# A seven-stage float32 block on one core: GpSimd's adds and most of its low parts go to VectorE, the opening follows the order of arrival, the softmax difference takes one pass

## The chip, the cores and the metric

The kernel runs on one core of one Trainium2 chip. The metric is the device time of one execution in microseconds (us), the median of several; the profile is one further execution with its own time. The engines are TensorE (PE, its weight loads PEld), VectorE (DVE), ScalarE (ACT), GpSimd (POOL) and SyncE (SP), which issues most of the transfers. Each engine works through its own list of instructions in order.

## The reference

One sequence of 256 positions and 1024 channels passes through seven residual stages. Matrix products are computed to float32 accuracy.

```python
h = h + 0.5 * g1 * swiglu(modulate(rmsnorm(h)))          # ffn1, 1024 -> 2816 -> 1024
h = h + g2 * hybrid_mixer(modulate(rmsnorm(h)))          # mixer: conv branch + gated delta rule
h = h + 0.5 * g3 * swiglu(modulate(rmsnorm(h)))          # ffn2
h = rmsnorm(h)
h = h + diff_attention(rmsnorm(h))                       # attn: softmax(a) - lam * softmax(b), 8 heads
h = h + mlp(rmsnorm(h)); h = h + mlstm(rmsnorm(h)); h = h + mlp(rmsnorm(h))
out = rmsnorm(h)
...
p = softmax(logits)                                      # diff_attention, per head
attn = p[:, 0] - lam * p[:, 1]
o = rmsnorm(attn @ v, subln_w) * 0.8                     # eps = 1e-6
```

## The kernel before, in words

`h` stays on chip with channels on the 128 partitions, as 8 tiles of 128x256. The weights (250 MB) stream in as 238 chunks of 1 MB, all issued on SP's queue (line 281), each into one of a few buffers named `raw`. A chunk is two halves of 128x1024. For each half `prep` makes a high part `whi` (ACT, line 320) and a low part `wlo = raw - whi` (line 323). Activations are split the same way (`xh`, `xl`), and each product is three matmuls: high by high (line 407), high weight by low activation (408), low weight by high activation (409). A "unit" is one half: 24 matmuls of 256 columns.

The order of the work on every engine is written out by the code as it runs: nothing is reordered later. `next` hands out a prepared half and prepares halves 2 ahead (4 ahead from `ffn2` on). The low part is recorded one step after the high part, on POOL or DVE: `self.st.pool` is 2 (both halves on POOL), 1 (the first half of each chunk on POOL) or 0 (all on DVE). A few halves at a stage's end (`now`) are always POOL's. Jobs of several steps (the delta rule, an attention core per pair of heads, the bias) sit in `side`; each unit calls `tick`, which takes one step of each job.

At the end of a stage `end_step` adds the products to `h` pair by pair, makes `xh` (ACT) and `xl` (DVE, line 706) for the next stage and squares `h` (ACT, line 625). POOL adds the squares into `ssum` (lines 626 and 628). The next stage starts its products (`unit_first`, line 448 for the `xl` part) before the norm is known; the sum's matmul stands late in the second group (`SUM`), the scale is spread by matmuls (line 668) in the fourth, and until then results are held.

In the mixer `dn_inverse` solves 32x32 triangles by forward substitution: 31 steps of two DVE instructions each (lines 1404 and 1406), two steps to a tick. In attention `combine` (lines 1053 to 1057) forms the difference of two softmaxes per head, and two ticks later `turn` transposes it on PE (line 1063). `h_settle` (line 2013) rescales `h` in eight DVE instructions at one place. In the opening `x` and the vectors come on ACT's queue while SP already loads weights; the norm of `x` must be known before the first product, since `first_ada` scales by it (line 552), and between them DVE reduces the first modulation column (`ada_tile`, line 531).

Of the kernel before, what the change touches and what calls it, by code (L numbers as in the profile page):

```python
# [18 lines left out]
P = 128  # L19
# [348 lines left out]
class Kern:  # L368
# [245 lines left out]
    def sq_start(self):  # L614
        self.ssum = self.work.tile([P, 2, S], F32, tag="ssum", name="ssum", bufs=1)

    def sq_add(self, j):

        nc = self.nc
        h = self.h[:, 2 * j:2 * j + 2]  # L620
        if j == 0:
            nc.scalar.activation(self.ssum, h, AF.Square)
            return
        sq = self.work.tile([P, 2, S], F32, tag="sq", name="sq", bufs=2)
        nc.scalar.activation(sq, h, AF.Square)  # L625
        nc.gpsimd.tensor_tensor(self.ssum, self.ssum, sq, op=ALU.add)  # L626
        if j == KT // 2 - 1:
            nc.gpsimd.tensor_tensor(self.ssum[:, 0], self.ssum[:, 0], self.ssum[:, 1], op=ALU.add)

    def norm_sum(self, parts=None):  # L630

        nc = self.nc
        if self.sqs is not None:
            return self.norm_sum2()
        ps = self.acc2()[:, 0]
        parts = parts or [self.ssum[:, 0]]
        if self.sq_out is not None:
# [113 lines left out]
    def group(self, fn):  # L751

        self.groups += 1
        self.held.append(fn)
        if self.groups <= self.spread_at and self.groups != SUM + 1:
# [260 lines left out]
    def attn_core(self, hp, q, k, bank):  # L1016
# [3 lines left out]
        mx = self.small.tile([P, 2, 4], F32, tag="mx", name="mx")  # L1020
        rec = self.small.tile([P, 2, 4], F32, tag="rec", name="rec")
        o = ap.tile([P, 2, S], F32, tag="o", name="o", bufs=3)
# [27 lines left out]

        def combine(i):
            t = pr[i]
            nc.vector.reciprocal(rec[:, i], sums[:, i])
            for b, c in parts:
                nc.vector.tensor_scalar(t[:, 1, c], t[:, 1, c], rec[:, i, 2 * b + 1:2 * b + 2], self.nlam,  # L1055
                                        op0=ALU.mult, op1=ALU.mult)
                nc.vector.scalar_tensor_tensor(t[:, 0, c], t[:, 0, c], rec[:, i, 2 * b:2 * b + 1], t[:, 1, c],  # L1057
                                               op0=ALU.mult, op1=ALU.add)
# [44 lines left out]
        c = self.small.tile([P, 4], F32, tag="c4", name="c4")  # L1103
        nc.vector.tensor_scalar(m, ms[:, :4], 1.0 / P, EPS, op0=ALU.mult, op1=ALU.add)
        self.rsqrt(c, m, 4)
# [13 lines left out]
    def attention(self, late):  # L1119
        nc = self.nc  # L1120
        x = (self.xh, self.xl)
        with ExitStack() as es:
# [6 lines left out]
            self.late()  # L1129
            self.st.pool = 2  # L1130
            self.v_done, self.down_on = set(), False
# [138 lines left out]
    def dn_keys(self):  # L1270
# [24 lines left out]
        for n in range(10):  # L1295
# [14 lines left out]
            if 1 <= n < 9:  # L1310
# [6 lines left out]
                kk[h] = self.scores(h, self.kqv[0][h // 2])  # L1317
            if n == 8:
                self.hold = False
                self.side.append(self.silu_rest())  # L1320
# [247 lines left out]
    def mixer(self, wide, wide_es, late):  # L1568
        nc = self.nc
        nm = "w_in"  # L1570
        with ExitStack() as es:
            self.mp = mp = es.enter_context(self.tc.tile_pool(name="mix", bufs=1))
            wba = self.work.tile([P, 2, S], F32, tag="sq", name="wba", bufs=2)[:, 0].rearrange("p (k c) -> p k c", k=KT)
            nc.scalar.dma_start(wba, self.arg["w_ba"])
            wb = self.work.tile([P, 2, S], F32R, tag="sq", name="wb", bufs=2).rearrange("p a (k c) -> p a k c", k=KT)
            wbh, wbl = wb[:, 0], wb[:, 1]
            self.zs = mp.tile([P, KT, S], F32, name="zs")
# [7 lines left out]
            for n in range(NLATE):  # L1585
# [12 lines left out]
                if n == 1:  # L1598
                    self.st.pool = 1
                if n == 3:  # L1600
# [13 lines left out]
            with self.tc.tile_pool(name="mix1", bufs=4) as m1:  # L1614
# [27 lines left out]
                def chain():  # L1642
# [3 lines left out]
                    self.side.append(self.dn_queries())  # L1646

                for r in (1, 0, 2):
                    for hp in range(4):
# [11 lines left out]
                self.tick_first = False  # L1661
                self.st.pool = 1
                for n in range(0, 8, 2):
# [213 lines left out]
    def mlstm(self, late):  # L1877
# [3 lines left out]
        with ExitStack() as es:  # L1881
# [78 lines left out]
            for n in range(8):  # L1960
# [6 lines left out]
                self.group(lambda ps=ps, c=4 * i + h, out=qk[h][i]: conv(ps, c, out))  # L1967
                if n == 1:
                    self.st.pool = 1
                if n == 3:  # L1970
# [5 lines left out]
            for h in range(4):  # L1976
                self.st.pool = 1
# [29 lines left out]
    def h_settle(self):  # L2007
# [3 lines left out]
        self.unsettled = False  # L2011
        for k in range(KT):
            self.nc.vector.scalar_tensor_tensor(self.h[:, k], self.h[:, k], self.vec("norm_final", k, 1), self.r1,
                                                op0=ALU.mult, op1=ALU.mult)

# [5 lines left out]
    def run(self):  # L2021
# [17 lines left out]
        c = self.small.tile([P, KT], F32, tag="c", name="c")  # L2039
        nc.sync.dma_start(c, arg["c"])  # L2040
        nc.scalar.dma_start(self.consts[:, :P], arg["consts"][:, :P])
        nc.scalar.dma_start(self.h, arg["x"])
        nc.scalar.dma_start(self.vecs, arg["vecs"])
# [6 lines left out]
        if "ffn1" in st:  # L2050
            self.zeros = self.first.tile([P, S], F32, name="zeros")
            nc.gpsimd.memset(self.zeros, 0.0)
            self.cold = self.acc2()[:, 0]
            self.warm(5)
        pc = [self.up(2 * S) for _ in range(2)]
# [3 lines left out]
        if "ffn1" in st:  # L2059
            sq = self.first.tile([P, 4, 2, S], F32, name="sq1")  # L2060
            h = self.h.rearrange("p (j a) s -> p j a s", a=2)
            for j in range(2):
                nc.scalar.activation(sq[:, j], h[:, j], AF.Square)
                nc.vector.tensor_tensor(sq[:, j + 2], h[:, j + 2], h[:, j + 2], op=ALU.mult)
            for j in (2, 0):
                nc.vector.tensor_tensor(sq[:, j], sq[:, j], sq[:, j + 1], op=ALU.add)
            for j in range(2):
# [5 lines left out]
            self.scale0 = self.first_scale()  # L2073
            self.norm_sum([sq[:, j, i] for j in (2, 0) for i in range(2)])
            self.warm(3)
# [157 lines left out]
```

## Time and profile before

| | |
|---|---|
| median of 3 runs | 1389.32 us (1383.68 to 1390.25) |
| the profiled execution's own time | 1393.07 us |
| its span (first to last instruction) | 1391.3 us |
| PE / DVE / ACT / POOL busy | 1339.4 / 979.2 / 665.9 / 202.0 us |
| mean granted TensorE clock | 0.980 of full speed |

Busy time is the union of an engine's instructions. A PE that is busy at half clock counts as busy, so the gap between PE's busy time and the span is not all that PE loses.

### The profile page before, as it was taken

The page shows a single profiled execution, that of the slowest core. Times are in us where ns is not written, and L with a number is a line of the kernel's source. Part 1 is how long each engine was busy: PE and PEld are TensorE (multiplying, and loading weights), DVE is VectorE, ACT ScalarE, POOL GpSimd, SP SyncE. Part 2 cuts the span into 40 slices and gives each one's busy share as a digit, 9 for nine tenths or more (in the row PEclk, how much of TensorE's full clock was granted, in tenths as well). Part 3 has the DMA queues.
Part 4 walks back from the last instruction along what each step waited for, and adds up shares of the span by engine and source line. Part 5 has one row for each costly group of instructions (what it writes and reads, how often), then busy time and mean ns, then how long its engine had stood idle before and what let it go on. Part 6 is the DMA issues. An engine that isn't in the chain of part 4 may idle for free.

```text
span 1391.3 us, 26555 instructions
## 1 busy us (share of the span) xinstructions
PE 1339.4 (96%) x11102; PEld 1312.1 (94%) x11102; DVE 979.2 (70%) x1757; ACT 665.9 (48%) x1052; POOL 202.0 (15%) x107
## 2 busy tenths in 40 slices
PE   8999999999989899999999989999999999999997
PEld 7999998999889899999999979999999899999997
DVE  6987778688797476965445886876665958866664
ACT  3544445657534435544445445544444664544442
POOL 0000004246224001000001653100000330100000
PEclk8999999999989999999999989999999999999998
DMA  8988763454547425486554432455555344455550
GB/s 326 360 298 305 305 275 113 137 179 152 152 156 216 175 89 185 156 318 213 186 185 139 147 121 100 153 181 182 182 183 182 122 152 167 145 204 182 182 182 31
DMA packets 44968, 257.97 MB, mean 185 GB/s; under 512 B 12520, under 2 KB 12784, under 8 KB 14256
## 3 DMA queue, kind: packets, MB, share of 16 engines
q1 hardware_dynamic: 34704, 250.10, 50.6%
q10 hardware_dynamic: 9760, 4.84, 1.6%
q8 instruction: 87, 1.43, 0.4%
q0 software_dynamic: 384, 1.32, 0.3%
q14 instruction: 33, 0.27, 0.1%
HBM read 254.14 MB, written 2.11 MB: 184 GB/s over the span
## 4 chain that ended last, share of the span: by engine, by line
PE 59%; DVE 8%; issue 0%; ACT 0%; DVEq 0%
PE up L407 10%; PE up L409 10%; PE up L408 10%; PE acc L407 7%; PE acc L409 7%; PE acc L408 7%; DVE xl L706 1%; DVE lt L1055 1%; PE acc L1523 1%; DVE wlo L323 1%; DVE lt L1057 1%; PE acc L668 1%; DVE xwl L706 0%; DVE h L833 0%; DVE rs_i L501 0%
## 5 line engine op out<-in xcount | busy, mean ns | idle before, releaser
L320 ACT CAST whi<-raw 128x1024 fp32r<-128x1024 f32 x404 | 420.7, 1047 | 437.4 <-PE up L408 184.3
L407 PE MATMUL up<-xh,whi 128*128 128x256 f32 x1744 | 504.7, 289 | 1.1 <-ACT xh L723 0.6
L409 PE MATMUL up<-xh,wlo 128*128 128x256 f32 x1744 | 497.3, 285 | 8.3 <-DVE wlo L323 8.3
L408 PE MATMUL up<-xl,whi 128*128 128x256 f32 x1744 | 497.0, 285 | 1.2 <-DVE xl L1720 1.1
L323 DVE TENSOR_TENSOR wlo<-raw,whi 128x1024 fp32r<-128x1024 f32 x337 | 420.4, 1258 | 68.4 <-ACT whi L320 66.5
L409 PEld LDWEIGHTS up<-xh,wlo 128*128 128x128 f32 x1744 | 337.6, 194 | 9.6 <-DVE wlo L323 9.5
L407 PEld LDWEIGHTS up<-xh,whi 128*128 128x128 f32 x1744 | 337.6, 194 | 3.9 <-issue 1.2
L408 PEld LDWEIGHTS up<-xl,whi 128*128 128x128 f32 x1744 | 337.6, 194 | 3.1 <-DVE xl L1720 1.3
L323 POOL TENSOR_TENSOR wlo<-raw,whi 128x1024 fp32r<-128x1024 f32 x67 | 164.9, 2463 | 667.3 <-ACT whi L320 657.2
L407 PE MATMUL acc<-gh,whi 128*128 128x256 f32 x864 | 244.7, 283 | 0.0
L409 PE MATMUL acc<-gh,wlo 128*128 128x256 f32 x864 | 244.6, 283 | 0.0
L408 PE MATMUL acc<-gl,whi 128*128 128x256 f32 x864 | 244.6, 283 | 0.0
L407 PEld LDWEIGHTS acc<-gh,whi 128*128 128x128 f32 x864 | 165.9, 192 | 0.6 <-issue 0.6
L408 PEld LDWEIGHTS acc<-gl,whi 128*128 128x128 f32 x864 | 165.9, 192 | 0.0
L409 PEld LDWEIGHTS acc<-gh,wlo 128*128 128x128 f32 x864 | 165.9, 192 | 0.0
L955 DVE TENSOR_TENSOR t<-up,rs 128x256 f32<-128x256 f32 x60 | 25.4, 423 | 103.5 <-PE up L409 103.5
L531 DVE SCALAR_TENSOR_TENSOR raw<-raw,crow 128x1024 f32<-128x1024 f32 x72 | 87.9, 1250 | 2.1 <-DMA raw<-in_stream 2.0
L882 DVE TENSOR_TENSOR gf<-up,sa 128x256 f32<-128x256 f32 x35 | 14.6, 423 | 79.2 <-PE up L409 79.2
L626 POOL TENSOR_TENSOR ssum<-ssum,sq 128x512 f32<-128x512 f32 x15 | 20.5, 1369 | 266.2 <-ACT sq L625 265.5
L878 ACT ACTIVATE sa<-up 128x256 f32<-128x256 f32 x35 | 13.3, 384 | 53.9 <-PE up L409 50.5
L407 PE MATMUL up<-whi,xh 128*128 128x256 f32 x128 | 38.8, 303 | 0.0
L408 PE MATMUL up<-wlo,xh 128*128 128x256 f32 x128 | 37.4, 292 | 0.0
(482 smaller groups left out, 1955.7 us busy)
## 6 DMA issues: line engine op xcount, KB each, us to landing
raw<-in_stream SPq DMA_DIRECT2D x238, 1024.0 KB, 5.0
h<-in_x ACTq DMA_DIRECT2D x1, 1024.0 KB, 8.4
bflip<-bdram POOLq DMA_DIRECT2D x1, 1024.0 KB, 6.7
d<-c ACTq DMA_DIRECT2D x1, 512.0 KB, 2.8
m<-d ACTq DMA_DIRECT2D x4, 128.0 KB, 7.0
d<-x ACTq DMA_DIRECT2D x1, 512.0 KB, 3.4
xd<-d ACTq DMA_DIRECT2D x4, 128.0 KB, 4.7
out_h<-h SPq DMA_DIRECT2D x2, 256.0 KB, 2.7
```

Of the source, the lines that this page charges most:

```text
L320: nc.scalar.copy(hi[:, :n], raw)
L323: self.lows.append(lambda: eng.tensor_tensor(lo[:, :n], raw, hi[:, :n].bitcast(F32), op=ALU.subtract))
L407: t.matmul(ps, lhsT=wh, rhs=xh, start=start, stop=False, skip_group_check=True)
L408: t.matmul(ps, lhsT=wh, rhs=xl, start=False, stop=False, skip_group_check=True)
L409: t.matmul(ps, lhsT=wl, rhs=xh, start=False, stop=stop, skip_group_check=True)
L531: self.nc.vector.scalar_tensor_tensor(w, w, 1.0, self.crow, op0=ALU.mult, op1=ALU.mult, accum_out=self.mods[:, c:c + 1])
L626: nc.gpsimd.tensor_tensor(self.ssum, self.ssum, sq, op=ALU.add)
L668: self.nc.tensor.matmul(ps[:, c0 + b * P:c0 + (b + 1) * P], lhsT=tok[:, b:b + 1].to_broadcast([P, P]), rhs=self.const("ident"), start=True ...
L706: nc.vector.scalar_tensor_tensor(x[1][:, k, :S], self.h[:, k], a[:, k:k + 1], x[0][:, k, :S].bitcast(F32), op0=ALU.mult, op1=ALU.subtract)
L882: product(n, lambda gf: None, lambda gf: nc.vector.tensor_tensor(gf, ps, sa, op=ALU.mult))
L955: nc.vector.tensor_tensor(t, src, self.rs, op=ALU.mult)
L1055: nc.vector.tensor_scalar(t[:, 1, c], t[:, 1, c], rec[:, i, 2 * b + 1:2 * b + 2], self.nlam, op0=ALU.mult, op1=ALU.mult)
```

## The change

The lambda of the softmax difference is multiplied by the ratio of the two sums, so that one pass forms the difference times the first sum; the factor is taken out by the norm that follows, whose eps is multiplied by that sum squared (`ep`). The squares of `h` are kept in four tiles (the fourth in PSUM) and added on DVE after the next stage's first group. `pool` is set only for the three q, k, v runs of the mixer (1), within `dn_keys` (2) and back to 0 at its ninth step. `h_settle` becomes a side job. In the opening `x` comes as two halves on SP's queue ahead of the weights, the squares and their sums follow the halves, and the first run of idle matmuls has 3 instead of 5. The small transfer `w_ba` is issued two groups later, since its buffer is one of the square tiles.

```diff
     def sq_add(self, j):
...
-        nc.gpsimd.tensor_tensor(self.ssum, self.ssum, sq, op=ALU.add)
-        if j == KT // 2 - 1:
-            nc.gpsimd.tensor_tensor(self.ssum[:, 0], self.ssum[:, 0], self.ssum[:, 1], op=ALU.add)
+        sq = self.ssum
+        if j == 3:
+            sq = self.acc2()
+        elif j:
+            sq = self.work.tile([P, 2, S], F32, tag="sq", name="sq", bufs=2)
+        self.nc.scalar.activation(sq, self.h[:, 2 * j:2 * j + 2], AF.Square)
+        self.sq_parts.append(sq)
+
+    def sq_sum(self):
...
+        add = lambda a, b: self.nc.vector.tensor_tensor(a, a, b, op=ALU.add)
+        a, b, c, d = self.sq_parts
...
+        add(a, b)
+        add(c, d)
+        add(a, c)
+        add(a[:, 0], a[:, 1])
...
         self.held.append(fn)
+        if self.groups == 1:
+            self.sq_sum()
...
         def combine(i):
...
-            nc.vector.reciprocal(rec[:, i], sums[:, i])
+            one = sums[:, i, 0:4:2]
+            nc.vector.reciprocal(rec[:, i], sums[:, i, 1:4:2])
+            nc.vector.scalar_tensor_tensor(rec[:, i], rec[:, i], self.nlam, one, op0=ALU.mult, op1=ALU.mult)
+            nc.vector.scalar_tensor_tensor(ep[:, i], one, EPS, one, op0=ALU.mult, op1=ALU.mult)
             for b, c in parts:
-                nc.vector.tensor_scalar(t[:, 1, c], t[:, 1, c], rec[:, i, 2 * b + 1:2 * b + 2], self.nlam,
-                                        op0=ALU.mult, op1=ALU.mult)
-                nc.vector.scalar_tensor_tensor(t[:, 0, c], t[:, 0, c], rec[:, i, 2 * b:2 * b + 1], t[:, 1, c],
+                nc.vector.scalar_tensor_tensor(t[:, 0, c], t[:, 1, c], rec[:, i, b:b + 1], t[:, 0, c],
                                                op0=ALU.mult, op1=ALU.add)
...
-        nc.vector.tensor_scalar(m, ms[:, :4], 1.0 / P, EPS, op0=ALU.mult, op1=ALU.add)
+        nc.vector.scalar_tensor_tensor(m, ms[:, :4], 1.0 / P, ep.rearrange("p a b -> p (a b)"),
+                                       op0=ALU.mult, op1=ALU.add)
...
-            self.st.pool = 2
             self.v_done, self.down_on = set(), False
...
             if n == 8:
+                self.st.pool = 0
                 self.hold = False
...
+                self.st.pool = 1
                 for r in (1, 0, 2):
...
-                self.st.pool = 1
                 for n in range(0, 8, 2):
...
-        for k in range(KT):
-            self.nc.vector.scalar_tensor_tensor(self.h[:, k], self.h[:, k], self.vec("norm_final", k, 1), self.r1,
-                                                op0=ALU.mult, op1=ALU.mult)
+
+        def settle():
+            for k in range(KT):
+                self.nc.vector.scalar_tensor_tensor(self.h[:, k], self.h[:, k], self.vec("norm_final", k, 1), self.r1,
+                                                    op0=ALU.mult, op1=ALU.mult)
+                yield
+        self.side.append(settle())
...
+        for j in range(2):
+            nc.sync.dma_start(self.h[:, 4 * j:4 * j + 4], arg["x"][:, 4 * j:4 * j + 4])
         nc.scalar.dma_start(self.consts[:, :P], arg["consts"][:, :P])
-        nc.scalar.dma_start(self.h, arg["x"])
...
-            self.warm(5)
+            self.warm(3)
```

How the lists of the engines change is seen at three places. Of the 67 low parts that POOL made, 17 stay there; DVE has 387 in place of 337.

The first place is DVE's list at the seam between attention and the first mlp, before: `h` and `xl` pair by pair, then low parts and the norm.

```order
L833 TENSOR_TENSOR h<-acc,h 128x512
L706 SCALAR_TENSOR_TENSOR xl<-h,vecs,xh 128x256 x4
L323 TENSOR_TENSOR wlo<-raw,whi 128x1024 x3
L644 TENSOR_SCALAR nm<-acc 128x2
L501 TENSOR_SCALAR rs_i<-nm 128x2
```

And of the change:

```order
L846 TENSOR_TENSOR h<-acc,h 128x512
L717 SCALAR_TENSOR_TENSOR xl<-h,vecs,xh 128x256 x4
L323 TENSOR_TENSOR wlo<-raw,whi 128x1024 x2
L632 TENSOR_TENSOR ssum<-ssum,sq 128x512
L632 TENSOR_TENSOR sq<-sq,acc 128x512
L632 TENSOR_TENSOR ssum<-ssum,sq 128x512
L632 TENSOR_TENSOR ssum<-ssum 128x256
L323 TENSOR_TENSOR wlo<-raw,whi 128x1024
L655 TENSOR_SCALAR nm<-acc 128x2
```

The four adds moved behind all of `xl` and two low parts, ahead of the norm; before, POOL made them while DVE made `xl`.

The second place is DVE's list in the middle of the forward substitution, before (`tmp` and `x` are its two instructions of a step, `ct` belongs to the convolution branch):

```order
L1406 TENSOR_TENSOR x<-x,tmp 128x16x16
L323 TENSOR_TENSOR wlo<-raw,whi 128x1024
L1404 TENSOR_TENSOR tmp<-m,x 128x255
L1406 TENSOR_TENSOR x<-x,tmp 128x15x17
L1404 TENSOR_TENSOR tmp<-m,x 128x252
L1406 TENSOR_TENSOR x<-x,tmp 128x14x18
L1691 TENSOR_TENSOR ct<-up,cc 128x256
L1404 TENSOR_TENSOR tmp<-m,x 128x247
```

And of the change:

```order
L1423 TENSOR_TENSOR x<-x,tmp 128x16x16
L323 TENSOR_TENSOR wlo<-raw,whi 128x1024
L1421 TENSOR_TENSOR tmp<-m,x 128x255
L1423 TENSOR_TENSOR x<-x,tmp 128x15x17
L1421 TENSOR_TENSOR tmp<-m,x 128x252
L1423 TENSOR_TENSOR x<-x,tmp 128x14x18
L1707 TENSOR_TENSOR ct<-up,cc 128x256
L323 TENSOR_TENSOR wlo<-raw,whi 128x1024
L1421 TENSOR_TENSOR tmp<-m,x 128x247
```

Between the first and the last of the 31 steps DVE now has 13 low parts, where it had 6.

The third place is DVE's list in attention where a pair of heads is combined, before (`rec` are reciprocals of the sums, `lt` the exponentials):

```order
L1156 TENSOR_TENSOR k<-up,rs 128x256
L1053 RECIPROCAL rec<-sums 128x4
L1055 TENSOR_SCALAR lt<-lt,rec,nlam 128x128
L1057 SCALAR_TENSOR_TENSOR lt<-lt,rec 128x128
L1055 TENSOR_SCALAR lt<-lt,rec,nlam 128x256
L1057 SCALAR_TENSOR_TENSOR lt<-lt,rec 128x256
```

And of the change:

```order
L1172 TENSOR_TENSOR k<-up,rs 128x256
L323 TENSOR_TENSOR wlo<-raw,whi 128x1024
L1069 RECIPROCAL rec<-sums 128x2
L1070 SCALAR_TENSOR_TENSOR rec<-rec,nlam,sums 128x2
L1071 SCALAR_TENSOR_TENSOR ep<-sums 128x2
L1073 SCALAR_TENSOR_TENSOR lt<-lt,rec 128x128
L1073 SCALAR_TENSOR_TENSOR lt<-lt,rec 128x256
```

Two passes over 128x128 and 128x256 are gone, two instructions on 128x2 are new, and a low part stands in nearly every unit.

## Rows read from the trace of the kernel before

**Rows 1.** The page, part 1: busy us, share of the span, instructions.

```profile
PE 1339.4 (96%) x11102; PEld 1312.1 (94%) x11102; DVE 979.2 (70%) x1757; ACT 665.9 (48%) x1052; POOL 202.0 (15%) x107
```

**Rows 2.** Waits of PE, whole span: us in total, times, longest.

```profile
PE up L409 <- DVE wlo L323: 9.3, 8, 4.2
PE acc L1063 <- DVE lt L1057: 5.8, 3, 3.8
...
PE acc L448 <- DVE xl L706: 3.1, 3, 1.0
PE acc L448 <- DVE xwl L706: 2.8, 4, 1.1
```

**Rows 3.** Waits of PE in 380 to 400, 400 to 420 and 1080 to 1120 us.

```profile
PE up L409 <- DVE wlo L323: 4.2, 1, 4.2
...
PE up L409 <- DVE wlo L323: 2.1, 1, 2.1
...
PE acc L668 <- DVE rtok L515: 1.6, 1, 1.6
```

**Rows 4.** Timeline: start, us, engine, line, operation; POOL's rows and DVE's.

```profile
801.03 2.41 POOL L323 TENSOR_TENSOR wlo<-raw,whi 128x1024 fp32r<-128x1024 f32 x1 [0.30 <-ACT whi L320]
...
801.12 2.47 DVE L1055 TENSOR_SCALAR lt<-lt,rec,nlam 128x256 f32<-128x256 f32 x1
...
847.22 0.41 DVE L1055 TENSOR_SCALAR lt<-lt,rec,nlam 128x256 f32<-128x256 f32 x1
...
888.68 0.87 DVE L706 SCALAR_TENSOR_TENSOR xl<-h,vecs,xh 128x256 fp32r<-128x256 f32 x2
889.47 0.68 DVE L833 TENSOR_TENSOR h<-acc,h 128x512 f32<-128x512 f32 x1
890.07 4.79 DVE L706 SCALAR_TENSOR_TENSOR xl<-h,vecs,xh 128x256 fp32r<-128x256 f32 x4
...
890.32 4.26 POOL L626 TENSOR_TENSOR ssum<-ssum,sq 128x512 f32<-128x512 f32 x3 [31.54 <-ACT sq L625]
```

**Rows 5.** Line 323 by source, DVE's group: ns min/median/max, first and last start.

```profile
L323 DVE TENSOR_TENSOR wlo<-raw,whi x337: 1202/1219/3422, 20.4 to 1365.1; 128x1024 fp32r<-128x1024 f32 x169
```

**Rows 6.** Timeline of DVE: first and last of seven in 363 to 416 us, of eighteen in attention.

```profile
363.95 2.38 DVE L1404 TENSOR_TENSOR tmp<-m,x 128x31 f32<-128x31 f32 x1
...
412.04 2.30 DVE L1406 TENSOR_TENSOR x<-x,tmp 128x60 f32<-128x60 f32 x1
...
764.00 1.46 DVE L660 TENSOR_SCALAR nm<-nm 128x2 f32<-128x2 f32 x1
...
856.51 2.41 DVE L1057 SCALAR_TENSOR_TENSOR lt<-lt,rec 128x128 f32<-128x128 f32 x1
```

**Rows 7.** Windows: us, busy of PE, PEld, DVE, ACT, POOL, granted clock, DMA.

```profile
363.00:416.00 53.00, 46.70 (x349) 45.96 (x348) 49.39 (x93) 21.13 (x34) 17.48 (x7) 0.90 0.45 159
756.00:864.00 108.00, 99.96 (x751) 95.20 (x750) 83.74 (x167) 52.26 (x125) 55.36 (x23) 0.92 0.38 127
...
559.90:563.40 3.50, 3.50 (x16) 3.50 (x17) 3.34 (x3) 0.73 (x1) 0.00 (x0) 0.51 0.41 96
805.70:812.50 6.80, 6.20 (x28) 5.48 (x29) 6.66 (x18) 0.48 (x1) 0.27 (x1) 0.50 0.46 154
833.00:836.40 3.40, 3.09 (x14) 2.80 (x15) 2.12 (x6) 0.48 (x1) 0.00 (x0) 0.50 0.21 89
10.40:20.60 10.20, 8.92 (x31) 7.91 (x32) 7.49 (x30) 2.96 (x6) 0.00 (x0) 0.50 0.91 350
```

**Rows 8.** The opening: transfers with us to landing, then timeline rows.

```profile
h<-in_x ACTq DMA_DIRECT2D x1, 1024.0 KB, 8.4
...
13.01 1.22 DVE L531 SCALAR_TENSOR_TENSOR raw<-raw,crow 128x1024 f32<-128x1024 f32 x1
15.29 0.16 DVE L644 TENSOR_SCALAR nm<-acc 128x2 f32<-128x2 f32 x1 [1.05 <-PE acc L641]
20.83 0.39 PE L407 MATMUL acc<-xh,whi 128*128 128x256 f32 x1
```

More of the change, by code (lines that the diff above doesn't have):

```diff
@@ L615, in sq_start @@
         self.ssum = self.work.tile([P, 2, S], F32, tag="ssum", name="ssum", bufs=1)
+        self.sq_parts = []
     def sq_add(self, j):
[L619 to L622, printed above, removed]
-            return
-        sq = self.work.tile([P, 2, S], F32, tag="sq", name="sq", bufs=2)
-        nc.scalar.activation(sq, h, AF.Square)
-        nc.gpsimd.tensor_tensor(self.ssum, self.ssum, sq, op=ALU.add)
-        if j == KT // 2 - 1:
-            nc.gpsimd.tensor_tensor(self.ssum[:, 0], self.ssum[:, 0], self.ssum[:, 1], op=ALU.add)
+        sq = self.ssum
[6 more added lines that the diff above has]
+    def sq_sum(self):
+        if len(self.sq_parts) < 4:
+            return
+        add = lambda a, b: self.nc.vector.tensor_tensor(a, a, b, op=ALU.add)
+        a, b, c, d = self.sq_parts
+        self.sq_parts = []
+        add(a, b)
+        add(c, d)
+        add(a, c)
+        add(a[:, 0], a[:, 1])
     def norm_sum(self, parts=None):
@@ L754, in group @@
         self.held.append(fn)
+        if self.groups == 1:
+            self.sq_sum()
         if self.groups <= self.spread_at and self.groups != SUM + 1:
@@ L1020, in attn_core @@
         mx = self.small.tile([P, 2, 4], F32, tag="mx", name="mx")
-        rec = self.small.tile([P, 2, 4], F32, tag="rec", name="rec")
+        rec = self.small.tile([P, 2, 2], F32, tag="rec", name="rec")
+        ep = self.small.tile([P, 2, 2], F32, tag="ep", name="ep")
         o = ap.tile([P, 2, S], F32, tag="o", name="o", bufs=3)
@@ L1572, in mixer @@
             self.mp = mp = es.enter_context(self.tc.tile_pool(name="mix", bufs=1))
[L1573 to L1576, printed above, removed]
             self.zs = mp.tile([P, KT, S], F32, name="zs")
@@ L1598, in mixer @@
                 if n == 1:
-                    self.st.pool = 1
+                    wba = self.work.tile([P, 2, S], F32, tag="sq", name="wba", bufs=2)[:, 0].rearrange("p (k c) -> p k c", k=KT)
+                    nc.scalar.dma_start(wba, self.arg["w_ba"])
+                    wb = self.work.tile([P, 2, S], F32R, tag="sq", name="wb", bufs=2).rearrange("p a (k c) -> p a k c", k=KT)
+                    wbh, wbl = wb[:, 0], wb[:, 1]
                 if n == 3:
@@ L1661, in mixer @@
                 self.tick_first = False
-                self.st.pool = 1
                 for n in range(0, 8, 2):
@@ L1967, in mlstm @@
                 self.group(lambda ps=ps, c=4 * i + h, out=qk[h][i]: conv(ps, c, out))
-                if n == 1:
-                    self.st.pool = 1
                 if n == 3:
@@ L1976, in mlstm @@
             for h in range(4):
-                self.st.pool = 1
                 pv = self.unit_wide(nm, x)
@@ L2061, in run @@
             h = self.h.rearrange("p (j a) s -> p j a s", a=2)
[L2062 to L2066, printed above, removed]
+            nc.scalar.activation(sq[:, 0], h[:, 0], AF.Square)
+            nc.vector.tensor_tensor(sq[:, 1], h[:, 1], h[:, 1], op=ALU.mult)
+            nc.vector.tensor_tensor(sq[:, 0], sq[:, 0], sq[:, 1], op=ALU.add)
+            nc.scalar.activation(sq[:, 2], h[:, 2], AF.Square)
+            nc.vector.tensor_tensor(sq[:, 3], h[:, 3], h[:, 3], op=ALU.mult)
+            nc.vector.tensor_tensor(sq[:, 2], sq[:, 2], sq[:, 3], op=ALU.add)
             for j in range(2):
@@ L2073, in run @@
             self.scale0 = self.first_scale()
-            self.norm_sum([sq[:, j, i] for j in (2, 0) for i in range(2)])
+            self.norm_sum([sq[:, j, i] for j in (0, 2) for i in range(2)])
             self.warm(3)
```

## The prediction

> **What bounds the kernel now.** I read the page first: PE is busy for 96% of the span and DVE for 70% [rows 1]. So the matmuls are the bound, and a change that leaves them alone can only give back what PE loses between them. That loss has two parts. The first is PE's waits. The view of waits names DVE behind most of them: for low parts 9.3 us, for the softmax difference 5.8, for the low parts of the new activations at the stage seams 3.1 and 2.8 [rows 2]. The second is the granted clock: after such waits there are stretches in which PE runs at 1.2 GHz instead of 2.4 [rows 7], and each us of them does half a us of work.
>
> DVE has 30% of its time free, so why is it late? The timeline answers. POOL starts a low part at 801.03 and needs 2.41 us; DVE starts a pass over 128x256 at 801.12, and it ends when POOL's ends, after 2.47 us [rows 4]. The same form takes 0.41 us at 847.22, beside no POOL work [rows 4]. At the seam behind attention two `xl` instructions take 0.87 us together, and the last four, beside POOL's three adds, 4.79 [rows 4]. A DVE instruction that reads its operands from SBUF and meets a POOL instruction there is held until POOL has finished. DVE is in order, so all behind it is late too. I take that as the mechanism: in 363 to 416 us seven DVE instructions are stretched so, by 12.5 us over their plain forms, and in attention eighteen, by 30.4 us [rows 6]. A low part costs DVE 1.22 us when it makes it itself [rows 5], half of what it can lose to POOL's.
>
> **The change part by part**, against the profiled execution's own 1393.07 us (span 1391.3).
>
> *Opening.* The last product before the steady run waits for the norm of `x`. `x` lands 8.4 us after its issue, the sums' result is used at 15.29, and the first product starts at 20.83 [rows 8]. Transfers ran at 350 GB/s [rows 7]. `x` shared this with the weights on SP's queue, so about 2.1 MB had to move before its last byte, 6.0 us, which leaves 2.4 us of start. Placed first on SP's queue it shares with constants and vectors alone, 1.05 + 0.38 MB, 4.1 us: an estimate of 6.5 in place of 8.4, 1.9 us earlier. The first half's square and add now lie beside the second half's transfer, so two of four DVE passes of about 0.68 us [rows 4] are out of the chain: 1.4 more. The first weight chunk comes later than before, 3.0 us behind `x`, at about 9.5 from the issue; DVE's pass over it, now at 13.01 [rows 8], still starts earlier. I take 3.3. The low end is 1: the clock is at 1.2 GHz from 10.4 to 20.6 us [rows 7] after PE had idled, and products that start sooner may start at that clock. The high end is 5, if `x` gets most of the rate. By the Trainium skill (TensorE: Matmul & The Clock Gate, What's actually happening) the gate throttles by default and activity releases it, which speaks against dropping two of the five idle matmuls; no row here shows a start with three, and by this rule the term would be at its low end.
>
> *Seams.* Five seams lose POOL's adds. Each had one wait of about 1.0 us for the last `xl`: three are the 3.1, two are in the 2.8, whose two other waits are short [rows 2]. The last four `xl` took 4.79 us where twice 0.87 is 1.74 [rows 4], so the last lands 3 us sooner and PE does not wait: 5.0 (3 to 5.9, which is all of both rows). The adds return as three passes of 0.68 and one of half that on DVE, 2.4 us, behind `xl` and ahead of the norm. That is less than the 3.0 freed just before, so the norm is not later; without that cover it would cost up to 2.4 at each seam. They wait for ACT's last square, which ACT makes straight behind the last `xh`; queued behind them are a low part two units ahead of its use and the norm. At the mLSTM's seam POOL also holds a DVE low part, and PE waits 1.6 us for the norm [rows 3]; I take 1.6 (0 to 1.6). Of the 9.3 us for low parts, 3.0 are small waits at other places, most behind a held DVE; I take 2 (0 to 3).
>
> *Substitution, 363 to 416 us.* DVE is busy for 49.39 of 53 us [rows 7], and PE waits 4.2 and 2.1 for low parts [rows 3]. Seven low parts come to DVE here, 7 x 1.15 = 8.0 us, and 12.5 us of holding go. DVE gains 4.5 us and PE follows DVE here, so I take 4.5. The bounds: -2, if half of the holding stays, and 6.3, both waits.
>
> *Attention, 756 to 864 us.* DVE is busy for 83.74 of 108 us [rows 7]. 23 low parts come, 23 x 1.15 = 26.4; the eight combines lose a pass over 128x256 (0.41, [rows 4]) and one over half of it, and gain two tiny instructions, about 3 us saved in all; 30.4 of holding go. That leaves about 77 us of DVE work for some 96 us of PE work, and the transposes have two ticks of slack behind the combine. Of the 5.8 us I take 5 (1 to 5.8). The eight `h_settle` instructions, one by one, cost the same DVE time; before, they stood as one block ahead of a combine.
>
> *Clock.* The stretches of 3.5, 6.8 and 3.4 us at 1.2 GHz [rows 7] follow the waits at the mixer's end and in attention that I take away: 13.7 us at half speed, 6.9 us of work. Not each goes with its wait; I take 5 (0 to 6.9). That of the substitution I leave out, as DVE is the bound there.
>
> *Nothing* for the earlier or later place of `w_ba` (one small transfer, two groups ahead of its use) and for squares written to PSUM: ACT is busy for 48% [rows 1].
>
> Sum: 3.3 + 5.0 + 1.6 + 2 + 4.5 + 5 + 5 = 26.4, to 1366.7 by the profiled execution. The median lies 3.75 below that execution, so I predict 1389.3 - 26.4 = 1363 us. The low ends add up to 3 us, the high ends to 34.5.
>
> **The rivals.**
>
> *DVE turns slow by its own load.* Where DVE is nearly full, the low parts only change their reason to be late: substitution and attention gain nothing, nor does the clock, and the opening, the seams and the mLSTM's norm give 9.9: 1379 us. For it speaks that DVE gets 50 low parts, 57 us, into stretches that are 93% and 78% full, and that low parts now stand ahead of the combine in DVE's list. Against it: the holding is larger than the load in both.
>
> *DVE becomes the bound, slower.* If the stretched instructions were late for a reason that stays, attention would hold 83.74 + 26.4 - 3 = 107 us of DVE work; with half of its old idle time, 12, that is 119 for 108, and the substitution 49.4 + 8 + 3.6 of idle = 61 for 53. Nineteen us lost against 9.9 gained: 1398. It decides once less than 64% of the holding goes in the substitution (8.0 of 12.5) and about three quarters in attention (23 of 30.4). For this speaks a rule of the Trainium skill (Perfetto Trace Analysis, Optimizing Scalar/DVE Operations): with DVE saturated, moving work to ScalarE or even GpSimd may make sense. The same section adds that the two share a read port and that it might not help, and that is what rows 4 show. So I give it little.
>
> *All goes.* The high ends give 34.5. If the substitution then runs at full clock too, 53 us at a granted 0.90 [rows 7] give another 5.3: about 1350. For it speaks that most waits have one cause; against it, that DVE stays 80% full in attention and in order.
>
> *The softmax difference does nothing by itself*: 3 us of DVE work in attention are hidden unless DVE is the bound there; it is no term of its own.
>
> **How the numbers follow.** Forecast, 1353 to 1372: 0.55. DVE slow by its own load, 1372 to 1383: 0.22. All goes, below 1353: 0.13. Slower: 0.05. No change for reasons that I don't see: 0.05. The range 1346 to 1379 leaves out the slower case, no change, half of the "all goes" and a part of the first rival, about 0.2. A measurement of this kernel can tell 0.5%, 7 us, from no change. Faster than that: 0.87 (the forecast, "all goes", most of the first rival); within it: 0.08; slower: 0.05.
>
> **What would show it.** Right: no DVE instruction at a seam or in attention above its plain length; POOL with 17 low parts; the first product near 17.5 us; no wait of PE for `xl` at the five seams; waits for `lt` under 1 us; fewer stretches at half clock. Wrong: DVE over 90% busy in attention, with PE waiting for `wlo` there; the substitution as long as before; the first product at 20 us, with `x` landed early but the first chunk of weights late. The prediction fails if DVE is not late because of POOL, or if the half clock stays where it is.

## Result and the profile after

| | before | after |
|---|---|---|
| median | 1388.34 us (1383.68 to 1390.25) | 1355.38 us (1355.24 to 1355.85) |
| profiled execution's own time / its span | 1393.07 / 1391.3 us | 1355.85 / 1354.1 us |
| mean granted TensorE clock | 0.980 | 0.989 |

The ratio is 0.9768 [0.9743, 0.9793]: 33 us less by the medians, 37.2 us less by the two spans. The forecast was 1363.

The page, part 1, of the kernel after (as [rows 1]):

```profile
PE 1320.2 (97%) x11098; PEld 1297.7 (96%) x11098; DVE 968.4 (72%) x1827; ACT 666.3 (49%) x1052; POOL 57.1 (4%) x37
```

DVE has 70 instructions more and is busy 11 us less, although it took over 50 low parts and the adds. Most of the stretching that was counted as its busy time is gone. Counted over the whole span are DVE's instructions that overlap one of POOL and last over 0.2 us longer than the median of the same form away from POOL: 63 before, 84.5 us above that median, and 13 after, 9.4 us. Of these 13, eight lie beside POOL's copies `L` at 412 to 422 us, in the mixer (2.8 us); no run here moves those copies.

To see where the time came from I split the executions at PE's landmarks: the first product of each stage, the first matmul of the mixer's gates (`pre_i`), the last matmul of its solve, the last transpose of a `turn`. Lengths in us, worked out from start times in the timeline; the four columns on the right are experiments told below.

| stretch | before | after | low parts alone | attention's back | mixer's back | adds back |
|---|---|---|---|---|---|---|
| start to first product | 20.8 | 16.9 | 20.7 | 16.7 | 16.5 | 15.9 |
| mixer to its gates | 53.7 | 48.0 | 50.2 | 48.0 | 52.1 | 51.6 |
| gates to the last solve (substitution, mixer's end) | 198.8 | 189.1 | 189.6 | 191.7 | 197.8 | 188.6 |
| ffn2 to attention | 200.9 | 198.2 | 200.9 | 198.2 | 198.2 | 199.6 |
| attention to the last turn | 110.0 | 96.7 | 97.1 | 103.0 | 96.7 | 93.7 |
| mlp0 to mLSTM | 186.9 | 187.1 | 186.9 | 187.1 | 187.1 | 186.9 |
| mLSTM to mlp1 | 116.6 | 114.5 | 114.3 | 114.5 | 114.5 | 114.3 |
| mlp1 to the last matmul | 192.7 | 192.9 | 192.7 | 192.9 | 193.2 | 192.6 |

Two of these stretches in the view of windows (columns as in [rows 7]), first of before, the mixer's middle and attention:

```profile
267.92:466.74 198.82, 185.07 (x1795) 178.07 (x1794) 150.41 (x301) 108.72 (x189) 79.02 (x39) 0.97 0.53 175
750.75:860.80 110.05, 102.01 (x769) 97.27 (x768) 85.36 (x167) 56.69 (x132) 55.36 (x23) 0.92 0.35 117
```

The same two of after:

```profile
258.24:447.33 189.09, 181.46 (x1795) 174.74 (x1795) 153.83 (x318) 108.91 (x189) 39.87 (x22) 0.98 0.55 181
728.61:825.33 96.72, 96.30 (x769) 93.15 (x768) 77.44 (x190) 56.74 (x132) 0.00 (x0) 0.96 0.42 139
```

In attention the same 769 matmuls now run with 0.4 us of idle PE in place of 8.0, and the clock is granted at 0.96 in place of 0.92. DVE has 23 instructions more there and is busy 7.9 us less.

The opening after, as in [rows 8] (transfers, then timeline rows):

```profile
h<-in_x SPq DMA_DIRECT2D x2, 512.0 KB, 5.4
...
10.23 1.23 DVE L531 SCALAR_TENSOR_TENSOR raw<-raw,crow 128x1024 f32<-128x1024 f32 x1 [0.98 <-DMA raw<-in_stream]
11.39 0.15 DVE L655 TENSOR_SCALAR nm<-acc 128x2 f32<-128x2 f32 x1
16.89 0.38 PE L407 MATMUL acc<-xh,whi 128*128 128x256 f32 x1
```

The sums are used at 11.39 instead of 15.29, and the first product starts at 16.89 instead of 20.83.

Not everything went. The longest waits of PE, whole span (as [rows 2]):

```profile
PE acc L652 <- DVE ssum L632: 3.4, 3, 1.1
PE acc L444 <- DVE h L850: 3.3, 2, 1.7
PE up L407 <- ACT whi L320: 3.1, 1, 3.1
```

The waits for `xl` at the seams (5.9 us in two lines of [rows 2]) are gone, and the first two lines here, 6.7 us, stand at the same five seams: for the sum at the three without a gate, for `h` at the two with one (behind ffn1 and the mixer, where the products are multiplied by a gate as they are added to `h`). DVE's timeline at the seam into mlp0 shows the first kind (compare [rows 4], where the last four `xl` took 4.79):

```profile
854.61 1.66 DVE L717 SCALAR_TENSOR_TENSOR xl<-h,vecs,xh 128x256 fp32r<-128x256 f32 x4
857.64 2.36 DVE L323 TENSOR_TENSOR wlo<-raw,whi 128x1024 fp32r<-128x1024 f32 x2 [1.37 <-ACT whi L320]
859.92 0.69 DVE L632 TENSOR_TENSOR ssum<-ssum,sq 128x512 f32<-128x512 f32 x1
...
861.96 0.42 DVE L632 TENSOR_TENSOR ssum<-ssum 128x256 f32<-128x256 f32 x1
```

`xl` is done 3.1 us sooner, but the next in DVE's list is a low part whose high part ACT has not made: DVE stands idle for 1.37 us, then makes two low parts, and only then adds the squares, the last of which ACT had finished at 856.64.

### The profile page after: what moved, and what is told of

It is laid out like the page before. It is cut to its first block, busy times and chain, and to the rows that moved or that the text cites. A ratio compares the mean times of both kernels' runs of the same rounds, so it can differ in the third digit from the quotient of the medians.

```text
span 1354.1 us, 26498 instructions
## 1 busy us (share of the span) xinstructions
PE 1320.2 (97%) x11098; PEld 1297.7 (96%) x11098; DVE 968.4 (72%) x1827; ACT 666.3 (49%) x1052; POOL 57.1 (4%) x37
## 4 chain that ended last, share of the span: by engine, by line
PE 84%; DVE 9%; ACT 3%; issue 1%; DMA 1%; ACTq 1%; SPq 0%; DVEq 0%
PE up L407 16%; PE up L409 16%; PE up L408 16%; PE acc L407 9%; PE acc L408 9%; PE acc L409 9%; DVE wlo L323 3%; DVE raw L531 1%; PE acc L1278 1%; PE acc L1540 1%; PE acc L679 1%; ACT xh L713 1%; ACT whi L320 1%; DVE ssum L632 0%; ACTq L1430 0%
## 5 line engine op out<-in xcount | busy, mean ns | idle before, releaser
L323 DVE TENSOR_TENSOR wlo<-raw,whi 128x1024 fp32r<-128x1024 f32 x387 | 470.1, 1224 | 68.2 <-ACT whi L320 66.1
L323 POOL TENSOR_TENSOR wlo<-raw,whi 128x1024 fp32r<-128x1024 f32 x17 | 41.0, 2416 | 389.9 <-ACT whi L320 383.8
L891 ACT ACTIVATE sa<-up 128x256 f32<-128x256 f32 x35 | 13.3, 384 | 50.9 <-PE up L409 47.5
L407 PE MATMUL acc<-yh,whi 128*128 128x256 f32 x128 | 36.4, 284 | 0.0
```

Source lines behind the costliest of these rows:

```text
L323: self.lows.append(lambda: eng.tensor_tensor(lo[:, :n], raw, hi[:, :n].bitcast(F32), op=ALU.subtract))
L407: t.matmul(ps, lhsT=wh, rhs=xh, start=start, stop=False, skip_group_check=True)
```

## The experiments

**Theory.** A GpSimd instruction that reads SBUF holds VectorE's until it ends, and that is most of the loss (A). **Rivals:** attention's gain comes from the softmax difference and the spread `h_settle` (B); the low parts only change their reason to be late and the rest of the change does the work (C). Ratios are to the kernel before; the changed kernel's 0.9768 is the yardstick.

### The low parts alone

On the kernel before, only the numbers of `pool` changed (the comments are added here; the second removed number stood at four places):

```diff
-            self.st.pool = 2          # attention
...
             if n == 8:
+                self.st.pool = 0
...
-                    self.st.pool = 1  # mixer's first product, gb, mLSTM
+                self.st.pool = 1      # mixer's q, k, v
```

> The kernel before with only the low parts moved from GpSimd to VectorE as in the changed kernel; opening, seam adds, softmax difference and h_settle stay as before. Theory A (a GpSimd instruction holds VectorE's, and that is most of the loss): the mixer between its opening gates and its end gives back about 13 us and attention about 12, so 1361 to 1366 us. Theory B (attention's gain comes from the softmax difference in one pass and from h_settle being spread out): only the mixer's part, 1373 to 1378 us. Theory C (the low parts only change their reason to be late, the rest of the change does the work): 1383 to 1389 us.

1364.50 us, ratio 0.9816 [0.9799, 0.9832]. As A has it (1361 to 1366): 50 low parts that change their engine give 25.8 us, where the whole change gives 33. Attention falls to 97.1 us with the old softmax difference and the old block of `h_settle`. Windows, attention:

```profile
737.81:834.89 97.08, 96.66 (x770) 93.49 (x769) 80.93 (x190) 56.85 (x132) 0.00 (x0) 0.96 0.40 136
```

C falls with this run, and so does B as it stands: attention's gain is there without the softmax difference and the spread `h_settle`.

### Attention's low parts back on GpSimd

```diff
+            self.st.pool = 2
             self.v_done, self.down_on = set(), False
```

> The changed kernel with attention's low parts back on GpSimd (pool = 2 there, one line). Theory A: attention's stretched VectorE instructions come back, and with them about 10 to 13 us: 1365 to 1369 us, with the turns' waits for lt and half-clock stretches in attention. Theory B: the softmax difference already relieves VectorE, so 0 to 3 us are lost: 1355 to 1359 us.

1363.47 us, 0.9806 [0.9792, 0.9821], between what A and B said. Windows, attention:

```profile
730.75:833.79 103.04, 98.72 (x770) 94.83 (x769) 79.97 (x167) 56.63 (x132) 55.62 (x23) 0.95 0.37 125
```

103.0 us: 6.3 more than the changed kernel, but 7.0 less than before, and A said 10 to 13. With the low parts on POOL the shorter `combine` and the spread `h_settle` do count; this run does not tell the two apart. The view of waits has 1.9 us for `lt` in place of 5.8.

### The softmax difference in two passes

```diff
...
-                nc.vector.scalar_tensor_tensor(t[:, 0, c], t[:, 1, c], rec[:, i, b:b + 1], t[:, 0, c],
+                nc.vector.tensor_scalar(t[:, 1, c], t[:, 1, c], rec[:, i, 2 * b + 1:2 * b + 2], self.nlam,
+                                        op0=ALU.mult, op1=ALU.mult)
+                nc.vector.scalar_tensor_tensor(t[:, 0, c], t[:, 0, c], rec[:, i, 2 * b:2 * b + 1], t[:, 1, c],
...
```

> The changed kernel with the softmax difference in two passes as before (reciprocals of all four sums, plain eps in the norm). Theory A: VectorE has room in attention once nothing holds it, so the 3 us of passes are hidden: 1355 to 1357 us, the same within the measurement. Theory B: the turns wait for lt again: 1363 to 1368 us.

1353.31 us, 0.9733 [0.9719, 0.9748], no slower than the changed kernel, and 1.7 us below the range that A gave. Windows, attention:

```profile
727.80:822.96 95.16, 94.74 (x770) 91.59 (x769) 80.96 (x190) 56.73 (x132) 0.00 (x0) 0.98 0.40 139
```

DVE is busy 3.5 us more and PE still idles 0.4. The 1.6 us in which attention is shorter go with the granted clock, 0.98 to 0.96.

### The mixer's low parts back on GpSimd

```diff
             if n == 8:
-                self.st.pool = 0
...
                 if n == 1:
+                    self.st.pool = 1
...
-                self.st.pool = 1
...
                 self.tick_first = False
+                self.st.pool = 1
```

> The changed kernel with the mixer's low parts back on GpSimd as before (from the second group of its first product to its end, attention stays changed). Theory A: the first product's part (about 5 us), the substitution (3) and the mixer's end (about 6) come back: 1366 to 1371 us. If the mixer's end was won by something else (the earlier part merely shifting what collides there), 1361 to 1364 us. If the low parts are no cause in the mixer at all, 1355 to 1357 us.

1366.84 us, 0.9824 [0.9798, 0.9849]. The median is as A has it; the four executions spread from 1360.47 to 1368.45, so the stretches carry the reading. The mixer's first part grows by 4.1 us and its middle by 8.7. Windows, that middle:

```profile
261.93:459.70 197.77, 185.56 (x1795) 178.73 (x1794) 150.52 (x301) 108.84 (x189) 78.58 (x39) 0.96 0.53 176
```

Waits of PE, whole span:

```profile
PE up L409 <- DVE wlo L323: 7.8, 6, 4.2
```

The wait of 4.2 us for a low part in the substitution [rows 3] is back, and the mixer's middle is as long as before, within about 1 us.

### GpSimd instructions that nothing needs

Both kernels are the changed one with an extra POOL instruction for each weight half prepared in attention, released by a one-column ACT copy.

```diff
...
+            def extra(hi):
+                nc.scalar.copy(scr[:, 0:1], hi[:, 0:1].bitcast(F32))
+                nc.gpsimd.tensor_tensor(scr[:, :D], scr[:, :D], scr[:, D:2 * D], op=ALU.mult)
...
```

> The changed kernel, and beside each weight half prepared in attention one more GpSimd instruction that nothing needs: a product of two 128x1024 pieces of a scratch tile, of the size of a low part, released by a one-column ScalarE copy. VectorE's list is that of the changed kernel. Theory A (a GpSimd instruction that reads SBUF holds VectorE's): some 20 stretched VectorE instructions come back at 1.2 us and more each, some 25 us of VectorE time; since VectorE also makes the low parts, that is more than it has free: attention 10 to 25 us longer, 1365 to 1380 us. If GpSimd does not hold VectorE (its low parts were late because GpSimd is slow): nothing waits for these instructions, 1355 to 1358 us.

1378.12 us, 0.9909 [0.9895, 0.9923]: 23 us lost by the medians, 20.3 of them in attention by the traces, to work that nobody waits for. Timeline, DVE's and POOL's rows:

```profile
782.39 2.41 POOL L1155 TENSOR_TENSOR scr<-scr 128x1024 f32<-128x1024 f32 x1 [3.59 <-ACT scr L1154]
782.71 3.18 DVE L324 TENSOR_TENSOR wlo<-raw,whi 128x1024 fp32r<-128x1024 f32 x1
...
785.66 2.46 POOL L1155 TENSOR_TENSOR scr<-scr 128x1024 f32<-128x1024 f32 x1 [0.86 <-ACT scr L1154]
785.81 0.15 DVE L1072 RECIPROCAL rec<-sums 128x2 f32<-128x2 f32 x1
786.00 2.14 DVE L1073 SCALAR_TENSOR_TENSOR rec<-rec,nlam,sums 128x2 f32<-128x2 f32 x1
```

The low part takes 3.18 us: POOL ends at 784.80, and 1.09 us later the low part is done, about its plain 1.22. The tiny `rec` ends at 788.14, POOL's at 788.12. The reciprocal between them, with one operand, passes at 0.15. Windows, attention:

```profile
730.58:847.60 117.02, 104.59 (x769) 99.66 (x768) 105.07 (x187) 61.05 (x155) 62.00 (x24) 0.90 0.32 109
```

DVE's busy time goes from 77.4 to 105.1 us by the holding alone, 90% of the stretch, and it is the bound there: of the 12.4 us that PE idles, 12.0 are waits for DVE. What has an operand in PSUM passes: of DVE's instructions there that overlap a product, 27 read `acc` or `up`, which are in PSUM, and none of them is stretched.

The second kernel has a write in place of the product:

```diff
-                nc.gpsimd.tensor_tensor(scr[:, :D], scr[:, :D], scr[:, D:2 * D], op=ALU.mult)
+                nc.gpsimd.memset(scr, 1.0)
```

> The same with a GpSimd instruction that only writes: a memset of the scratch tile, 128x2560 elements, about 2.4 us by the memset of 128x1024 in the trace. If it is GpSimd's reading of SBUF that holds VectorE: 1355 to 1358 us, no stretched instruction. If any GpSimd access holds it: as with the products, 1365 to 1380 us.

1355.95 us, 0.9751 [0.9732, 0.9770], the same as without. Timeline:

```profile
792.65 2.24 POOL L1155 MEMSET scr<- 128x2560 f32 x1 [2.66 <-ACT scr L1154]
793.45 0.22 DVE L1073 SCALAR_TENSOR_TENSOR rec<-rec,nlam,sums 128x2 f32<-128x2 f32 x1
...
796.18 2.24 POOL L1155 MEMSET scr<- 128x2560 f32 x1 [1.30 <-ACT scr L1154]
796.59 1.86 DVE L504 TENSOR_SCALAR rs_i<-m 128x4 int32<-128x4 int32 x1
```

`rec` beside a memset takes its plain 0.22. Of the 125 instructions of DVE that overlap a memset in attention, 19 of them low parts, three are stretched, all of them `TENSOR_SCALAR`s: the one shown, which ends at 798.45 with the memset (798.42), and two at 743.37 (1.89 us) and 745.50 (2.28 us), which end with theirs too. "No stretched instruction" was therefore not quite right.

The Trainium skill (SBUF — State Buffer, Who interferes with whom) says that VectorE and GpSimd share one pair of ports as an exclusive lock: a VectorE instruction with two SBUF inputs contends with a GpSimd one that reads, not with one that only writes; one with a single input does not contend unless it can run in a two-port mode, as `tensor_scalar` can. The five rows of DVE shown agree: `wlo` and `rec` held by the product, the reciprocal free, `rec` free beside the memset, the `TENSOR_SCALAR` held by it.

### The old opening

The changed kernel with `x` as one transfer on ACT's queue, the old order of the squares and five idle matmuls.

```diff
-        for j in range(2):
-            nc.sync.dma_start(self.h[:, 4 * j:4 * j + 4], arg["x"][:, 4 * j:4 * j + 4])
...
+        nc.scalar.dma_start(self.h, arg["x"])
...
-            self.warm(3)
+            self.warm(5)
...
```

> The changed kernel with the opening as before (x in one transfer on ACT's queue, squares and sums in the old order, five idle matmuls). If the opening's 3.9 us in the landmarks are its own and nothing later absorbs them: 1358.5 to 1360 us. If a later stage takes up the shift (the time of the next weights decides): 1355 to 1357 us.

1360.78 us, 0.9790 [0.9772, 0.9808], just above the first range. The first product is at 21.2, 4.3 us later, and the mixer still starts 3.9 us later. The interval of the ratio overlaps that of the changed kernel, so the landmarks tell it better than the medians.

### GpSimd's adds back

```diff
...
-        self.sq_parts.append(sq)
...
+        nc.gpsimd.tensor_tensor(self.ssum, self.ssum, sq, op=ALU.add)
...
```

> The changed kernel with GpSimd's adds of the squares at the five seams as before. By the step on record (five waits for xl of 1 us go, and nothing comes in their place): 1360 to 1361.5 us, with the waits for xl back. By the new waits read in the trace of the changed kernel (for the sum at three seams, for h at two, about as long as the old ones): 1355 to 1358 us.

1358.90 us (1355.38 to 1362.28), 0.9779 [0.9757, 0.9801]: between the two ranges, and the interval overlaps that of the changed kernel, so the medians do not decide. Waits of PE, whole span:

```profile
PE acc L448 <- DVE xl L720: 3.1, 3, 1.0
PE acc L448 <- DVE xwl L720: 2.8, 4, 1.0
```

The old waits are back and the new ones gone. In the 20 us around each seam, PE's waits of 0.2 us or more come to 7.4 us over the five with these adds and to 8.0 in the changed kernel. By the waits alone the adds on DVE gave nothing.

The stretches (last column of their table) say otherwise. Behind the two gated seams the mixer's first part is 3.6 us longer than in the changed kernel and ffn2 is 1.4 us longer; behind the three without a gate the stages are 0.2 to 0.3 us shorter. That makes 4.3 us for the adds on DVE, 1.7 of which are half of a stretch of 3.4 us at half clock, at 219.6 in the mixer of this run. The kernel with the low parts alone, which has the old adds too, gives 4.2 in the same way (2.2 and 2.7, less 0.7 at the other three). It repeats elsewhere: with the adds on POOL ffn2 takes 199.6 to 200.9 us (this run, the low parts alone, before), and 198.0 to 198.4 in the changed kernel and the six experiments above that keep its seams. The view of waits does not hold all that PE loses at a gated seam; what else it loses there stays open. The last matmul ends 0.4 us earlier in this profile than in that of the changed kernel only because the opening is 1.0 and attention 3.0 us shorter, with less time at half clock, and these adds have no part in either.

### The fourth square's bank, and the place of the adds

Two causes were read from the trace. At the gated seams the next stage's second result needs a bank of `acc`; the fourth square took the free one, so that result waits for the bank of the last `h`. At the others the adds stand behind low parts. First the bank alone:

```diff
         if j == 3:
-            sq = self.acc2()
+            sq = self.up2()
```

> The changed kernel with the fourth square in a bank of the other PSUM pool (up2 in place of acc2). If the two waits for h at the gated seams (1.9 and 2.0 us) come from the bank that this square takes from the next stage's second result, they go: 1351.5 to 1353.5 us. If PE waits there for the last h itself, nothing changes: 1355 to 1356 us.

1356.70 us, 0.9764 [0.9744, 0.9784]: no gain, and just above both ranges. The waits for `h` are gone at all seams, and those for the sum are longer. PE's waits:

```profile
PE acc L652 <- DVE ssum L632: 5.0, 3, 1.7
PE acc L679 <- DVE rtok L515: 4.4, 3, 2.4
```

PE reaches the sum's matmul sooner, and the sum is as late as it was. The bank was one cause of two in a row. By the stretches the mixer's first part is 0.8 us shorter than in the changed kernel, and mLSTM and mlp1 are 1.5 us longer each, each with a stretch of 3.4 us at half clock (at 1047.0 and 1163.1) that the changed kernel does not have. With the adds ahead of the low parts as well:

```diff
         self.flush(True)
+        self.sq_sum()
         self.st.low()
```

> The same, and the four adds recorded straight behind the last xl, ahead of the low parts that wait for ACT. If the sum is late at three seams because the adds stand behind these low parts, its waits (1.1 us each, 3.4 in all) go as well: about 3 us below the run with the bank alone, 1348.5 to 1351 us. If the adds then delay the low parts that PE needs next, as much comes back there: no gain over the bank alone, with waits for wlo in the second group.

1352.48 us, 0.9732 [0.9712, 0.9753], less gain than expected. The three seams without a gate have no wait of PE left, while at the two gated ones PE waits 2.0 us each for a low part that now stands behind the adds (the mixer's first part takes 50.6 us, ffn2 200.1). So the last kernel puts them early only where there is no gate:

```diff
         self.flush(True)
+        if self.add_early:
+            self.sq_sum()
         self.st.low()
...
+        self.add_early = gate is None and late is not None
```

> The bank of the other pool, and the adds ahead of the low parts only at the three seams without a gate; at the two gated ones they stay behind the first group. By the waits read in the two runs before, the seams then hold 1.5 us of PE's waits in place of 8.0 in the changed kernel: 6.5 us less, 1348 to 1350.5 us if the half-clock stretches stay as they are. If the early adds at the ungated seams only move the wait to a low part or the norm, 1352 to 1355 us.

1347.85 us, 0.9699 [0.9684, 0.9713], 7.5 us below the changed kernel, and the intervals do not meet. The five stages behind the seams are shorter than in the changed kernel by 0.8, 0.0, 1.8, 1.8 and 1.8 us. In the 20 us around each seam one wait of PE is left, at ffn2:

```profile
PE acc L679 <- DVE rtok L515: 1.5, 1, 1.5
```

### The last 17 low parts on VectorE

```diff
-            eng = nc.gpsimd if self.pool > half or now else nc.vector
+            eng = nc.vector
```

> The changed kernel with the last 17 low parts on VectorE too (pool ignored, also for the halves at a stage's end). By theory A they hold VectorE in the mixer's q, k, v products and at the seams, and VectorE is not full there: 1351 to 1355 us. If VectorE's load decides there (low parts at a seam stand in front of h and xl), 1357 to 1363 us.

1357.58 us, 0.9761 [0.9745, 0.9776], the same as the changed kernel, above the range that A gave and in that of the other theory. The mixer's middle takes 191.8 us where the changed kernel has 189.1 and other kernels with equal low parts there 189 to 192. ffn1, and the stretch from the last solve to ffn2, are 1.2 and 1.3 us longer, the mixer's first part and ffn2 0.8 and 0.9 shorter. Taking these holders away and giving VectorE their work thus cancel out here; whether VectorE's load is what decides, as that theory says, this run does not show.

## Why the prediction was right, and where it was not

The mechanism was right: GpSimd holds VectorE, and with the low parts and the adds gone from it most of the holding went. The median fell 8 us below the forecast, in its range. One step failed, at the seams, and the term came out near its size by luck. The terms, in us of the two profiled executions:

| term | forecast | measured | read from |
|---|---|---|---|
| opening | 3.3 | 3.9 | first product; 4.3 by the run with the old one |
| adds at the five seams (forecast as waits for `xl`) | 5.0 | 4.3 | the stages behind the seams, by the run with the adds back |
| mLSTM's norm | 1.6 | 2.1 | mLSTM to mlp1 |
| other low parts | 2 | 4 | the mixer's first part, by its low parts put back |
| substitution, and the mixer's end, which was left out | 4.5 | 9.7 | gates to the last solve |
| attention, waits and its clock | 5 + 5.1 | 13.3 | attention to the last turn |

The forecast's clock term of 5 is spread over the stretches here; the 5.1 are half of the 6.8 and 3.4 us of [rows 7] in attention. The rows of the table overlap at the seams and are not a sum.

*Opening.* Right in size. `x` was used from 6.04 on in halves, as said, the second half at 7.69, 1.9 us before the whole of it in the kernel before (9.60), and the first weights were late by 0.98 us of DVE's idle time only. The stretch at half clock fell from 10.2 us to 6.8 (windows, after):

```profile
9.40:16.20 6.80, 6.80 (x22) 5.59 (x23) 5.33 (x25) 1.19 (x2) 0.00 (x0) 0.51 1.01 425
```

Two idle matmuls fewer cost no clock here, and neither reason for the low end appeared.

*Seams: the step that failed.* The waits for `xl` went, as said. But "That is less than the 3.0 freed just before, so the norm is not later" took DVE's freed time as usable, and it was not. Ahead of the adds in DVE's list stand two low parts, and the first of them waits for ACT, so the 3.1 us became idle time and low parts. At the seam into mlp0 the adds ended at 9.9 us from the stage's start, where POOL's had ended at 7.5 with the last of its four (timeline of before, behind the three of [rows 4]):

```profile
894.65 0.79 POOL L628 TENSOR_TENSOR ssum<-ssum 128x256 f32<-128x256 f32 x1
```

So new waits came in place of the old ones, 8.0 us for 7.4. The sentence that squares in PSUM cost nothing priced ACT's time and left out the bank. Both are shown by the last two kernels on the bank and the adds: in the last, 6.5 us of the 8.0 go and the time falls by 7.5. That the term is 4.3 for a forecast of 5.0 is luck. The forecast was 1.0 at each seam; the stretches give 3.6 and 1.4 at the two gated ones, 1.7 of it half clock, and a loss of 0.2 to 0.3 at each of the other three.

*mLSTM's norm.* Right in size, but the adds were not its cause: with the low parts alone the stretch is already at 114.3 us.

*Substitution and mixer's end.* Undersized. I left out the end because PE waits for ACT there, 2.7 and 1.3 us. From the gates to the inverse's first matmul the changed kernel gains 3.0 us, from there to the last solve 6.7. In the last version of the seams the same 50 low parts are moved, and it is 7.0 and -0.1, with two waits for ACT of 2.8 and 1.4 us at the same place. So the sum of the two stretches follows the low parts (7 to 10 us in all kernels that move them, 1 where the mixer's are put back), and the split between them is set by something else; what that is stays open.

*Attention.* Undersized. I priced one line of waits, 5.8 us for `lt`. The window has 8.0 us of idle PE, and 7.6 of it went; the clock gave about 5 of the remaining 5.7, from 0.92 over 110 us to 0.96 over 97.

*Clock.* Span times what the mean clock lacks of full speed is 27.8 us before (0.980) and 14.9 after (0.989), 12.9 of the 37.2, where 5 were forecast. The three stretches that I named are gone, but so are stretches in the opening, in the mixer's first part and in its middle. The one of 3.5 us that I put down to the mixer's end lies 10 us behind ffn2's first product; it is still there with the low parts alone (3.4 us at 547.4), so the waits that I named did not make it.

*The rivals.* DVE slow by its own load: in attention it is busy for 77.4 of 96.7 us, and no turn waits for `lt`. DVE the bound: with the useless products it was, at 90% busy, so this rival was possible; it did not come because the holding went. The softmax difference does nothing by itself: right as it stands in the changed kernel, wrong where POOL still holds DVE (up to 7.0 us together with `h_settle`).

*The signs.* All those named for right came but one: none of DVE's instructions in attention is above its plain length, but at each gated seam one `xwl` is, beside a low part that POOL still makes (1.40 and 1.47 us for 0.48).

## What to carry to other kernels

An engine with idle time can be late because another holds its instructions: look for the same form at two lengths in the timeline, and whether the long ones end when the other engine's do. Such help can cost more than the work it takes over: in attention 30.4 us of holding stood against 23 low parts of 1.22 us. A helper that only writes cost next to nothing here, and VectorE's instructions with an operand in PSUM were not held. A view of waits can stay equal while a stage gets shorter: compare the lengths of the stages as well, and know what the clock did in them. When work is moved into time that was freed, read what the next instruction in that list waits for, and which buffer the moved work takes, since the time is only there if nothing else is late in front of it.

## What was not expected of the hardware

The holding depends on the form, not on the size: a `rec` of 128x2 elements was held for 1.9 us, while a reciprocal of the same size passed in 0.15. A memset of POOL left two-operand instructions alone and held three `TENSOR_SCALAR`s, one of 128x4 integers for 1.7 us. The holding goes the other way too: four of POOL's 23 products started while DVE was making a low part, took 3.05 to 3.42 us where the median is 2.41, and ended 2.2 to 2.3 us after that low part.
